# Splitting the preparation of the attention's values into prompt columns and a late sample step, in a hybrid decoder step on one Trainium2 core

## The chip, the cores and the metric

The kernel runs on one core of one Trainium2 chip. The metric is device time in microseconds (us). Engines are named as in the profile: PE is TensorE, DVE is VectorE, ACT is ScalarE, POOL is GpSimd, and SP only issues DMAs here. Each engine works through its own instructions in order, and semaphores tie the engines together. What is timed is one launch of the whole program.

## What is computed

One layer of a decoder for 1024 prompt tokens and 8 sample tokens (1032 columns in all; the samples are the last eight):

```python
hp, gate_p = _modulate(xp, c_prompt, w_cond[l], b_cond[l])
q, k, v, g_att, u, g_ssm, m_att, m_ssm = _project_in(hp, w_in[l])
o_att = _sb_prompt(q, k, v, sb_bias[l])                  # samples: _stick_breaking over a paged cache
y_ssm, sr, si = _ssm_branch(u, g_ssm, ...)               # ends in a GLU and @ w_ssm_out
# _finish:
y_att = (o_att.reshape(bsz, s, D_ATT) * jax.nn.silu(g_att)) @ w_att_out
merged = jax.nn.sigmoid(m_att) * y_att + jax.nn.sigmoid(m_ssm) * y_ssm
return _layer_norm(DEEPNORM_ALPHA * x + gate * (merged @ w_out), ln_g, ln_b)
```

The change concerns the left factor of the product with `w_att_out`: attention output times SiLU gate, which has to stand in SBUF, split in a high and a low part, before that product begins.

## The kernel before

All big products run as *jobs*: 128 output features for all 1032 columns, 8 input tiles x 3 column chunks of 344 x 3 products of high and low parts, 72 matmuls (L141, tile `pj`). A job takes the first and last two input tiles chunk by chunk, so its first 18 matmuls use tiles 0 and 1, the next 36 tiles 2 to 5, the last 18 tiles 6 and 7. The order on PE is written out by hand: `Stream.weave` spreads a list of small steps evenly over the jobs that are queued (down to a remainder `until`), and calls each step between two matmuls. The order on the other engines is left to the framework's scheduler, which goes by the order in which the code emits instructions and by its own estimate of times.

The end of the kernel has four phases of PE work: GLU (8 jobs), `ssm_out` (8 jobs), `att_out` (8 jobs) and `finish` (9 row blocks, L1397). Between them stand these pieces.

- *Late values* (`LateValues`): four of the eight cache pages of the samples' attention are weighted and summed here, in 34 steps. Step n (n < 32) loads tile `l_t` number n: DVE copies one element of the newest result into the tile (L865, so that the load does not start early), POOL issues an indirect DMA of 512 KB (L866). It then works up tile n-2: a DVE product (L884) and a DVE sum (L885). The last step adds the partial sums (L888) and ACT's queue writes the samples' attention output to `d_o` in DRAM (L889). NLATE steps are woven into the GLU, the others into `ssm_out` until LATE jobs are left of it: before 26 steps, then 8 steps over the first three jobs.
- *Gate steps* (`gate_steps`, 8 of them, over `ssm_out`): a product with a part of `w_cond` (L343, tile `gp`) whose operand is loaded into a `wc` tile (L327), split by ACT (L334, `wchi`) and by DVE (L335, `wclo`). Step n loads part n+2 and splits part n+1.
- *`open_a`* (8 steps, L1276 to L1289): for each of 8 feature tiles, load two halves of the attention output (`x` and `olo`, L1278) and the gate (`sga`, L1279), add (L1280), multiply (L1281); load the samples' rows from `d_o` (`orow`, L1283, SP's queue), transpose them on PE (`otp`, L1285), multiply (L1286); then split all 1032 columns (ACT L234, DVE L235). The gate steps and these steps are woven together over the last five jobs of `ssm_out`.
- Tiles `l_t`, `wc`, `olo`, `sga` (and `w_out` tiles later) share one ring of four SBUF buffers, tag `wc`: a tile can be loaded when the tile four allocations before it is used up. Tile `x` has a ring of two.
- Weights of the next job are loaded by SP's queue (L105), rounded by ACT (L108) and their low part made by POOL (`wlo`, L109). The results of `ssm_out` leave PSUM by DVE (L1261), those of the GLU by ACT (L1243) and DVE (L1244) and are then split (L234, L235).

Of the kernel before, what the change touches and what calls it, by code (L numbers as in the profile page):

```python
# [9 lines left out]
F32 = mybir.dt.float32  # L10
F32R = mybir.dt.float32r
I32 = mybir.dt.int32
AF = mybir.ActivationFunctionType
ALU = mybir.AluOpType
# [3 lines left out]
NP, NS, NT = 1024, 8, 1032  # L18
NC3, CW = 3, 344
KT = 8  # L20
# [8 lines left out]
MM = 146.0  # L29
# [4 lines left out]
HURRY = 400  # L34
# [3 lines left out]
QUEUES = "sasssasss"  # L38
PACE = 155
VP = 4  # L40
NLATE = 26
GS = "v"
LATE = 5.0
AHEAD = 2
DRAIN = 1.6
TWO_PI = 6.283185307179586
# [35 lines left out]
def blk(i, w=128):  # L82
    return slice(w * i, w * i + w)
# [141 lines left out]
def weaved(a, b):  # L225

    n = [((i + 0.5) / len(x), j, s) for j, x in enumerate((a, b)) for i, s in enumerate(x)]
    return [s for _, _, s in sorted(n, key=lambda e: e[:2])]


def split_act(k, pool, src):
    hi = pool.tile([128, NT], F32R, tag="hi", bufs=KT, name="ahi")
    lo = pool.tile([128, NT], F32R, tag="lo", bufs=KT, name="alo")
    k.nc.scalar.copy(hi, src)  # L234
    k.nc.vector.tensor_tensor(lo, src, hi.bitcast(F32), ALU.subtract)  # L235
    return hi, lo
# [301 lines left out]
class Attention:  # L538
# [130 lines left out]
    def turn(self, p, h, m, j):  # L669

        k, nc, pool = self.k, self.k.nc, self.pool
        PE, ACT, DVE = nc.tensor, nc.scalar, nc.vector
        w = [self.w[p, h, 2 * m + e][0] for e in range(2)]
        tp = self.ps.tile([128, 4, 128], F32, tag="wt", name="tp")
        if j < m:
            hi, lo = (pool.tile([128, 4, 128], F32R, tag=n, bufs=LAG + 1, name=n) for n in ("wthi", "wtlo"))
        else:
            hi, lo = self.diag
        order = (0, 1) if j < m else (1, 0)
        for a in order:  # L680
            for e in range(2):
                if j < m or (a, e) != (1, 0):
                    PE.transpose(tp[:, 2 * order[a] + e], w[e][:, blk(2 * j + a)], k.ident)  # L683
        with k.tc.high_priority(HURRY):
            s = slice(0 if j < m else 1, 4)
            ACT.copy(hi[:, s], tp[:, s])  # L686
            DVE.tensor_tensor(lo[:, s], tp[:, s], hi[:, s].bitcast(F32), ALU.subtract)  # L687
        return hi, lo
# [501 lines left out]
class Merge:  # L1190
# [77 lines left out]
    def open_a(self):  # L1268

        k, nc = self.k, self.k.nc  # L1270
        self.a_guard = self.pool("seta", "right")
        pa = self.a_guard.__enter__()
        self.act_a = []

        def one(f):
            t = self.load(k.d_a[f, 0], "x", NP)  # L1276
            o, s = (self.ld.tile([128, NP], F32, tag="wc", bufs=4, name=n) for n in ("olo", "sga"))
            nc.sync.dma_start(o, k.d_a[f, 1])  # L1278
            nc.sync.dma_start(s, k.d_sa[f])  # L1279
            nc.vector.tensor_tensor(t[:, 0:NP], t[:, 0:NP], o, ALU.add)  # L1280
            nc.vector.tensor_tensor(t[:, 0:NP], t[:, 0:NP], s, ALU.mult)  # L1281
            ob = self.ld.tile([NS, 128], F32, tag="orow", bufs=2, name="orow")
            nc.sync.dma_start(ob, k.d_o[:, blk(f)])  # L1283
            tp = k.psg.tile([128, 512], F32, tag="g", name="otp")
            nc.tensor.transpose(tp[:, 0:NS], ob, k.ident[0:NS, 0:NS])  # L1285
            nc.vector.tensor_tensor(t[:, NP:NT], tp[:, 0:NS], k.sgs[:, f], ALU.mult)  # L1286
            self.act_a.append(split_act(k, pa, t))

        return [(110, None, lambda f=f: one(f)) for f in range(KT)]  # L1289

    def att_out(self):
        k, nc = self.k, self.k.nc
# [160 lines left out]
def stickbreak_s5_kernel(ctx: ExitStack, tc: tile.TileContext, io, out):  # L1453
    nc = tc.nc
    k = Ctx()
# [55 lines left out]
    S = k.stream = Stream(k)  # L1511
# [108 lines left out]
    mg = Merge(k, io, out)  # L1620
# [8 lines left out]
    late = lv.steps()  # L1629
    S.weave(late[:NLATE])  # L1630
    S.drain()
    mg.g_guard.__exit__(None, None, None)
    mg.open_gate()
    mg.ssm_out()
    S.weave(late[NLATE:], LATE * KT * 9 * MM)
    S.weave(weaved(mg.gate_steps(), mg.open_a()))
    mg.s_guard.__exit__(None, None, None)
    mg.att_out()
    mg.open_out()
# [60 lines left out]
def build(nc, arrays):  # L1700
    from concourse import mybir as _mybir
    io = {n: nc.dram_tensor("in_" + n, v.shape, _mybir.dt.from_np(v.dtype), kind="ExternalInput").ap()
          for n, v in arrays.items()}
    out = {n: nc.dram_tensor("out_" + n, s, F32, kind="ExternalOutput").ap() for n, s in _OUTS}
    with tile.TileContext(nc, schedule_with_timeline_sim=True) as tc:
        stickbreak_s5_kernel(tc, io, out)
# [12 lines left out]
```

## Time and profile before

| | us |
|---|---|
| median of 3 runs (lowest to highest) | 1623.29 (1622.94 to 1626.74) |
| profiled execution, time | 1634.07 |
| profiled execution, span from first to last instruction | 1632.4 |

In the profiled execution PE is busy 92% of the span, DVE 75%, POOL 56%, ACT 45%. Times below count from the start of the span. A row of a timeline reads: start, duration, engine, line, operation, out<-in; in brackets the time in which the engine stood idle before it and what ended that. `PEclk` is the clock that PE was granted, 1.00 being 2.4 GHz and 0.50 1.2 GHz.

### The profile page before, as it was taken

Reading aid. Unit: us, or ns where it says so; the run is one execution under the profiler, and the core shown is the slowest. Engines: PE = TensorE matmul, PEld = TensorE weight load, DVE = VectorE, ACT = ScalarE, POOL = GpSimd, SP = SyncE. Lnnn points to the kernel's source line nnn. Section 1 sums busy time; section 2 is a strip of 40 time slices with the busy share of each in tenths; the row PEclk is TensorE's granted clock in tenths of the full one; section 3 lists DMA queues with packets and bytes.
Section 4 is the critical chain, followed back from the end, with each engine's and each line's share of the span. In section 5 each row is a group of like instructions: output and inputs, shape, how many; then the busy total and the mean of one; then the engine's idle time right before and its main releaser. Section 6 shows DMA issues by size and latency. Waiting matters only on the chain.

```text
span 1632.4 us, 25533 instructions
## 1 busy us (share of the span) xinstructions
PE 1496.4 (92%) x9321; PEld 1416.0 (87%) x9321; DVE 1220.2 (75%) x1717; ACT 737.4 (45%) x1360; POOL 909.0 (56%) x744
## 2 busy tenths in 40 slices
PE   8899999999999999999899898987988785999997
PEld 4689999999999999999889798987788785899885
DVE  4558888888888888734989888786489985844566
ACT  3557777777677767633333333333432212311200
POOL 1738787868787777564655555572276540132164
PEclk9999999999999999999999999998999987999999
DMA  9323433334343434347988878773556677854322
GB/s 348 108 87 86 105 102 96 100 95 113 94 113 87 119 92 106 116 142 246 289 282 258 290 231 268 264 234 80 161 169 195 211 257 256 329 190 144 116 79 91
DMA packets 176731, 275.47 MB, mean 169 GB/s; under 512 B 46395, under 2 KB 119867, under 8 KB 176477
## 3 DMA queue, kind: packets, MB, share of 16 engines
q1 hardware_dynamic: 150555, 180.40, 36.2%
q0 software_dynamic: 23456, 84.95, 16.1%
q10 hardware_dynamic: 2594, 8.49, 1.9%
q8 instruction: 73, 1.20, 0.3%
q14 instruction: 53, 0.43, 0.1%
HBM read 196.77 MB, written 66.24 MB: 161 GB/s over the span
## 4 chain that ended last, share of the span: by engine, by line
PE 48%; DVE 23%; DMA 10%; issue 6%; ACT 3%; SPq 3%; POOL 3%; DVEq 0%; POOLq 0%; ACTq 0%
PE pj L141 30%; PE f L1397 6%; PE o L700 4%; PE z L654 3%; DVE s_sc L828 3%; PE tp L683 3%; DVE ke L665 3%; DVE vs L636 2%; DVE be L666 2%; DMA tt<-gtt 1%; DVE s_t L823 1%; DMA l_t<-in_cache_v,l_idx 1%; SPq L956 1%; POOL l_t L866 1%; DMA s_t<-in_cache_k,s_idx 1%
## 5 line engine op out<-in xcount | busy, mean ns | idle before, releaser
L141 PE MATMUL pj<-ahi,whi 128*128 128x344 f32 x2112 | 698.9, 332 | 47.8 <-ACT u L970 20.3
L141 PE MATMUL pj<-alo,whi 128*128 128x344 f32 x2112 | 689.3, 328 | 7.9 <-DVE alo L1220 4.7
L141 PE MATMUL pj<-ahi,wlo 128*128 128x344 f32 x2112 | 584.2, 329 | 9.2 <-POOL wlo L109 9.2
L141 PEld LDWEIGHTS pj<-ahi,whi 128*128 128x128 f32 x2112 | 408.4, 193 | 56.8 <-ACT u L970 21.3
L141 PEld LDWEIGHTS pj<-alo,whi 128*128 128x128 f32 x2112 | 408.5, 193 | 12.2 <-DVE alo L1220 5.6
L141 PEld LDWEIGHTS pj<-ahi,wlo 128*128 128x128 f32 x2112 | 384.7, 193 | 11.4 <-POOL wlo L109 9.9
L665 DVE TENSOR_TENSOR_SCAN ke<-ke,eye 128x896 f32<-128x896 f32 (+7 forms) x128 | 219.6, 1716 | 92.9 <-ACT ke L655 92.8
L109 POOL TENSOR_TENSOR wlo<-w,whi 128x1024 fp32r<-128x1024 f32 x53 | 135.6, 2559 | 220.4 <-ACT whi L108 220.0
L108 ACT CAST whi<-w 128x1024 fp32r<-128x1024 f32 x90 | 94.9, 1054 | 130.1 <-PE pj L141 98.5
L655 ACT ACTIVATE ke<-z,nhb 128x448 f32<-128x448 f32 (+2 forms) x192 | 111.9, 583 | 81.3 <-PE z L654 79.3
L666 DVE TENSOR_TENSOR be<-be,ke 128x896 f32<-128x896 f32 (+7 forms) x128 | 120.5, 941 | 12.9 <-ACT wthi L686 0.5
L828 DVE SCALAR_TENSOR_TENSOR s_sc<-s_t,s_q,s_sc 128x512 f32<-128x512 f32 x126 | 109.8, 871 | 17.8 <-DMA s_t<-in_cache_k,s_idx 11.7
L656 ACT ACTIVATE be<-z,hb 128x448 f32<-128x448 f32 (+2 forms) x192 | 110.7, 577 | 0.0
L807 POOL DMA_INDIRECT s_t<-in_cache_k,s_idx x64 | 71.4, 1115 | 39.2 <-issue 11.4
L683 PE MATMUL tp<-ident,be 128*128 128x128 f32 x576 | 88.9, 272 | 0.0
L493 POOL TENSOR_TENSOR pt<-tab 128x256 f32<-128x256 f32 x64 | 79.1, 1236 | 3.1
L1520 ACT ACTIVATE gate<-pj 128x344 f32<-128x344 f32 x72 | 33.0, 460 | 101.2 <-PE pj L141 92.0
L492 POOL TENSOR_TENSOR pr<-tab 128x256 f32<-128x256 f32 x32 | 28.2, 880 | 90.3 <-DMA tab<-d_tab 75.7
L109 DVE TENSOR_TENSOR wlo<-w,whi 128x1024 fp32r<-128x1024 f32 x37 | 63.0, 1703 | 15.0 <-ACT whi L108 15.0
L686 ACT CAST wthi<-tp 128x512 fp32r<-128x512 f32 x96 | 56.7, 591 | 33.1 <-PE tp L683 30.8
L687 DVE TENSOR_TENSOR wtlo<-tp,wthi 128x512 fp32r<-128x512 f32 x96 | 65.4, 681 | 6.7 <-ACT wthi L686 6.5
L654 PE MATMUL z<-kl,qs 128*128 128x448 f32 (+2 forms) x192 | 66.2, 345 | 4.0 <-DMA kl<-kl 4.0
(314 smaller groups left out, 2764.8 us busy)
## 6 DMA issues: line engine op xcount, KB each, us to landing
w<-in_w_in SPq DMA_DIRECT2D x38, 512.0 KB
w<-in_w_in POOLq DMA_DIRECT2D x26, 512.0 KB, 6.2
wc<-in_w_cond SPq DMA_DIRECT2D x24, 512.0 KB
d_a<-ox SPq DMA_DIRECT2D x128, 64.0 KB
gst<-d_gg SPq DMA_DIRECT2D x8, 576.0 KB
x<-in_xr SPq DMA_DIRECT2D x9, 512.0 KB
xt<-in_xt SPq DMA_DIRECT2D x8, 516.0 KB
d_ma<-gate SPq DMA_DIRECT2D x8, 516.0 KB
```

Of the source, the lines that this page charges most:

```text
L108: nc.scalar.copy(whi, w32)
L109: self.eng.tensor_tensor(wlo, w32, whi.bitcast(F32), ALU.subtract)
L141: PE.matmul(ps[c], w[:, blk(t)], x[:, cs(c)], start=(t == 0 and i == 0), stop=(t == KT - 1 and i == 2))
L493: POOL.tensor_tensor(t1, c, d, ALU.mult)
L654: nc.tensor.matmul(z[:, 0:wide], st["q", h][:, blk(i)], x[:, s:s + wide], start=j == 0, stop=j == 1)
L655: nc.scalar.activation(ke[:, s:s + cw], z[:, 0:cw], AF.Sigmoid, bias=k.nhb[:, hd:hd + 1], scale=-0.125)
L656: nc.scalar.activation(be[:, s:s + cw], z[:, 0:cw], AF.Sigmoid, bias=k.hb[:, hd:hd + 1], scale=0.125)
L665: nc.vector.tensor_tensor_scan(rev, rev, self.eye[:, NP - n:][:, ::-1], 0.0, ALU.mult, ALU.add)
L666: nc.vector.tensor_tensor(be, be, ke[:, 1:n + 1], ALU.mult)
L683: PE.transpose(tp[:, 2 * order[a] + e], w[e][:, blk(2 * j + a)], k.ident)
L828: DVE.scalar_tensor_tensor(sc, t, q[:, d - d0:d - d0 + 1], sc, op0=ALU.mult, op1=ALU.add)
L1397: PE.matmul(pp[c], a[:, token(i)], w[:, blk(c, 512)], start=(t == 0 and a is ah and w is wh), stop=(t == KT - 1 and a is al))
```

## The change

`open_a` makes only the 1024 prompt columns. A new function `samples_a` makes the eight sample columns of all eight tiles: one load of `d_o` into a tile of the `wc` ring, eight transposes into one PSUM tile, one product, and sixteen small splits. Its load is emitted when 1.6 jobs of `ssm_out` are left, its transposes when 0.8 job is left. NLATE goes from 26 to 20, and the 14 late steps that remain are woven together with the gate steps and the prompt steps over the first 6.4 jobs of `ssm_out` (LATE from 5.0 to 1.6).

```diff
-NLATE = 26
+NLATE = 20
-LATE = 5.0
+LATE = 1.6
@@
-        def one(f):
-            t = self.load(k.d_a[f, 0], "x", NP)
+        def prompt(f):
+            t = self.load(k.d_a[f, 0], "x", NP)[:, 0:NP]
             o, s = (self.ld.tile([128, NP], F32, tag="wc", bufs=4, name=n) for n in ("olo", "sga"))
             nc.sync.dma_start(o, k.d_a[f, 1])
             nc.sync.dma_start(s, k.d_sa[f])
-            nc.vector.tensor_tensor(t[:, 0:NP], t[:, 0:NP], o, ALU.add)
-            nc.vector.tensor_tensor(t[:, 0:NP], t[:, 0:NP], s, ALU.mult)
-            ob = self.ld.tile([NS, 128], F32, tag="orow", bufs=2, name="orow")
-            nc.sync.dma_start(ob, k.d_o[:, blk(f)])
-            tp = k.psg.tile([128, 512], F32, tag="g", name="otp")
-            nc.tensor.transpose(tp[:, 0:NS], ob, k.ident[0:NS, 0:NS])
-            nc.vector.tensor_tensor(t[:, NP:NT], tp[:, 0:NS], k.sgs[:, f], ALU.mult)
-            self.act_a.append(split_act(k, pa, t))
-
-        return [(110, None, lambda f=f: one(f)) for f in range(KT)]
+            nc.vector.tensor_tensor(t, t, o, ALU.add)
+            nc.vector.tensor_tensor(t, t, s, ALU.mult)
+            hi = pa.tile([128, NT], F32R, tag="hi", bufs=KT, name="ahi")
+            lo = pa.tile([128, NT], F32R, tag="lo", bufs=KT, name="alo")
+            nc.scalar.copy(hi[:, 0:NP], t)
+            nc.vector.tensor_tensor(lo[:, 0:NP], t, hi[:, 0:NP].bitcast(F32), ALU.subtract)
+            self.act_a.append((hi, lo))
+
+        return [(0, None, lambda f=f: prompt(f)) for f in range(KT)]
+
+    def samples_a(self):
+
+        k, nc = self.k, self.k.nc
+        ob = self.ld.tile([NS, NP], F32, tag="wc", bufs=4, name="orow")
+        nc.sync.dma_start(ob, k.d_o)
+        tp = k.psg.tile([128, 512], F32, tag="g", name="otp")[:, 0:64].rearrange("p (f s) -> p f s", f=KT)
+        t = self.ld.tile([128, KT, NS], F32, tag="orow", bufs=1, name="os")
+
+        def turn():
+            for f in range(KT):
+                nc.tensor.transpose(tp[:, f], ob[:, blk(f)], k.ident[0:NS, 0:NS])
+            with k.tc.high_priority(HURRY):
+                nc.vector.tensor_tensor(t, tp, k.sgs, ALU.mult)
+                for f in range(KT):
+                    hi, lo = (x[:, NP:NT] for x in self.act_a[f])
+                    nc.scalar.copy(hi, t[:, f])
+                    nc.vector.tensor_tensor(lo, t[:, f], hi.bitcast(F32), ALU.subtract)
+
+        return [(900, None, turn)]
@@
-    S.weave(late[NLATE:], LATE * KT * 9 * MM)
-    S.weave(weaved(mg.gate_steps(), mg.open_a()))
+    S.weave(weaved(late[NLATE:], weaved(mg.gate_steps(), mg.open_a())), LATE * KT * 9 * MM)
+    S.weave(mg.samples_a())
```

Worked out from `weave`, in jobs of `ssm_out` from its start: before, the last late step comes at 2.67, the gate steps at 3.29, 3.88 and so on to 7.41, the first `open_a` step (and with it the first transpose) at 3.59. After, the gate steps come at 0.21, 1.03, 1.86 and so on to 5.78, the prompt steps at 0.62, 1.45 and so on to 6.19, the late steps at 0.41, 0.83 and so on to 5.99, and the transposes of the samples at 7.2.

## Rows read from the trace of the kernel before

**Rows 1.** Who waited for whom, PE alone, 1190 to 1540: total, times, longest

```profile
PE otp L1285 <- DMA orow<-d_o: 17.7, 1, 17.7
PE pj L141 <- POOL wlo L109: 9.2, 2, 4.9
PE pj L141 <- ACT ahi L234: 6.7, 1, 6.7
PE gp L343 <- DVE x L1286: 3.2, 1, 3.2
PE gp L343 <- DVE wclo L335: 1.7, 2, 1.1
```

**Rows 2.** Busy time by stretch: stretch, length, busy (instructions) per engine, PEclk, DMA share, GB/s

```profile
1196.00:1292.60 96.60, 87.40 (x514) 86.83 (x513) 92.73 (x96) 23.14 (x33) 61.81 (x35) 0.91 0.56 178
1292.60:1352.70 60.10, 45.32 (x266) 44.04 (x264) 50.80 (x64) 9.83 (x11) 23.62 (x17) 0.89 0.80 260
1352.70:1430.20 77.50, 62.32 (x351) 58.45 (x352) 51.53 (x62) 21.75 (x22) 10.31 (x4) 0.89 0.83 298
1430.20:1520.60 90.40, 90.40 (x577) 90.40 (x577) 38.39 (x41) 15.82 (x15) 24.36 (x8) 1.00 0.50 164
1520.60:1632.40 111.80, 101.17 (x436) 81.38 (x434) 71.87 (x147) 8.90 (x16) 46.40 (x33) 0.97 0.26 88
```

**Rows 3.** Timeline of PE where `ssm_out` meets the GLU's last split

```profile
1301.66 0.32 PE L141 MATMUL pj<-ahi,wlo 128*128 128x344 f32 x1
1308.72 0.66 PE L141 MATMUL pj<-ahi,whi 128*128 128x344 f32 x1 [6.75 <-ACT ahi L234]
```

**Rows 4.** Timeline of PE around its longest wait

```profile
1344.65 0.32 PE L141 MATMUL pj<-alo,whi 128*128 128x344 f32 x1
1344.80 0.48 PE L141 MATMUL pj<-ahi,wlo 128*128 128x344 f32 x2
1362.98 0.27 PE L1285 MATMUL otp<-ident,orow 8*128 8x8 f32 x1 [17.71 <-DMA orow<-d_o]
...
1363.64 0.49 PE L141 MATMUL pj<-ahi,whi 128*128 128x344 f32 x1
1363.92 0.49 PE L141 MATMUL pj<-alo,whi 128*128 128x344 f32 x1
...
1366.58 0.32 PE L141 MATMUL pj<-ahi,wlo 128*128 128x344 f32 x1
1366.73 0.32 PE L141 MATMUL pj<-ahi,whi 128*128 128x344 f32 x1
```

**Rows 5.** Timelines of POOL, DVE, ACT and SP: the last late load to the samples' rows

```profile
1340.95 0.94 POOL L866 DMA_INDIRECT l_t<-in_cache_v,l_idx  x1 [0.74 <-DVE l_t L865]
...
1352.50 0.22 DVE L888 TENSOR_TENSOR l_acc<-l_acc 128x64 f32<-128x64 f32 x1
...
1352.75 0.33 ACTq L889 DMA_DIRECT2D d_o<-l_acc  x1
...
1358.80 0.63 SPq L1283 DMA_DIRECT2D orow<-d_o  x2
```

**Rows 6.** By line, all or most of the trace: count, duration min/median/max ns, first to last start

```profile
L884 DVE TENSOR_TENSOR l_t<-l_t,l_sc x32: 1207/1214/8223, 1204.1 to 1349.0; 128x1024 f32<-128x1024 f32 x32
L1280 DVE TENSOR_TENSOR x<-x,olo x8: 1212/1224/3417, 1355.4 to 1422.2; 128x1024 f32<-128x1024 f32 x8
L1261 DVE TENSOR_TENSOR m<-pj,m x24: 498/508/517, 1311.1 to 1431.0; 128x344 f32<-128x344 f32 x24
L1285 PE MATMUL otp<-ident,orow x8: 223/223/271, 1363.0 to 1426.5; 8*128 8x8 f32 x8
L1219 ACT CAST ahi<-ygs x8: 197/235/347, 1157.1 to 1187.9; 128x8 fp32r<-128x8 f32 x8
L1220 DVE TENSOR_TENSOR alo<-ygs,ahi x8: 104/156/2405, 1158.1 to 1192.0; 128x8 fp32r<-128x8 f32 x8
```

**Rows 7.** Late products (L884) by stretch, columns as in group 2, DVE alone

```profile
1196.00:1292.60 96.60, 31.73 (x18) 0.91 0.56 178
1292.60:1352.70 60.10, 22.28 (x14) 0.89 0.80 260
```

**Rows 8.** Timelines of DVE, SP, PE: the gate's first operand, and loads through the ring

```profile
1289.68 1.20 DVE L885 TENSOR_REDUCE l_acc<-l_t 128x8 f32<-128x1024 f32 x1
...
1313.85 0.38 SPq L327 DMA_DIRECT2D wc<-in_w_cond  x1
...
1322.63 1.21 DVE L335 TENSOR_TENSOR wclo<-wc,wchi 128x1024 fp32r<-128x1024 f32 x1
...
1340.73 0.40 PE L343 MATMUL gp<-wchi,csplit 128*128 128x512 f32 x1
...
1349.58 0.37 SPq L1278 DMA_DIRECT2D olo<-d_a  x1
...
1391.07 0.38 SPq L327 DMA_DIRECT2D wc<-in_w_cond  x1
...
1414.63 0.32 SPq L1279 DMA_DIRECT2D sga<-d_sa  x1
```

**Rows 9.** Timeline of POOL ahead of the first wait of PE for `wlo`

```profile
1232.42 0.97 POOL L866 DMA_INDIRECT l_t<-in_cache_v,l_idx  x1 [4.05 <-DVE l_t L865]
1233.70 1.31 POOL L866 DMA_INDIRECT l_t<-in_cache_v,l_idx  x1 [0.31 <-issue]
1235.03 2.35 POOL L109 TENSOR_TENSOR wlo<-w,whi 128x1024 fp32r<-128x1024 f32 x1
```

## The prediction

> **What bounds the kernel now.** I read the waits of PE first, then the busy time by stretch, then the timelines around the longest wait. In the last 440 us PE hardly stands still except in five places, and one is far the longest: 17.7 us before the first transpose of the samples' rows [rows 1]. The stretches say what that is worth. From 1430.2 on (`att_out`, eight jobs in 90.4 us, so 11.3 us each) PE is busy without a gap, and in `finish` it is busy for 101 of 112 us [rows 2]: whatever brings the start of `att_out` forward brings the end forward by as much. Before it, in 1196 to 1292.6 (the GLU), PE is busy for 87.4 of 96.6 us and DVE for 92.7, so there DVE has hardly any slack; in 1292.6 to 1430.2 (`ssm_out`) PE has 107.6 of 137.6 us and DVE 102.3 [rows 2]. I place the start of `ssm_out` at 1292.6 because 57 matmuls of its first job, 0.157 us apart (90.4 us for the 576 of eight jobs), fit in before the wait that ends at 1308.72 for the GLU's last split [rows 3]; 57 is where tile 7 is first used.
>
> The timeline shows how the long wait comes about. PE's order reaches the first transpose at 1345.3, but DVE adds the last late partial sums only at 1352.5, ACT's queue writes `d_o` at 1352.75, SP's queue issues the load of the rows at 1358.80, and PE goes on at 1362.98 [rows 4, 5]. The order by hand assumed the late values done at 2.67 jobs; on the chip DVE was some 20 us late. Behind the transpose everything on PE is queued, though `ssm_out` does not need the samples.
>
> **The change part by part.**
>
> *The wait goes from its place.* Gone are 17.7 us, the 3.2 us in which a gate product waits for a PSUM bank held by a transpose's product (L1286), and the two short waits for `wclo` (1.7 us) that follow from the same crowding [rows 1]: 22.6 us. After the long wait nine matmuls run 0.29 us apart, at the lower level of the clock (1.2 GHz), not 0.157 us as before it and from 1366.6 on [rows 4], which is another 1.2 us; with a little of the same behind the 3.2 us wait it makes 24.5 us. If nothing took its place, `att_out` would start at 1430.2 - 24.5 = 1405.7.
>
> *The samples' step.* Eight transposes at 0.22 us (as before, so no difference), one DVE product, sixteen small splits. The nearest rows are the GLU's sample columns of the same size: 0.235 us on ACT and 0.156 us on DVE [rows 6], so 8 x 0.235 = 1.9 us of ACT with DVE following. They run beside 0.8 job (9.0 us) of `ssm_out` matmuls and are needed 12 matmuls into `att_out`; hidden, and about 4 us if that cover went. DVE loses eight products of 0.155 us and gains about as much: nothing.
>
> *What the transposes wait for now.* PE meets them at 7.2 jobs. Let T be the end of the last late sum. From T to the first transpose took 1362.98 - 1352.7 = 10.3 us [rows 5]; then come 1.8 us of transposes and 9.0 us of matmuls, so `att_out` starts at T + 21.1 or at 1405.7, whichever is later. Everything hangs on T, which the change puts behind more work: the last late step moves from 2.67 to 5.99 jobs, with seven of the eight prompt steps and all gate steps emitted ahead of it.
>
> *T by DVE's work.* DVE was busy for 92.73 + 50.80 = 143.5 us from 1196 to T [rows 2]. Of the 51.5 us after it, nearly all now stands ahead of T, but for one prompt step (3 x 1.22), the PSUM exits of the last two jobs (6 x 0.51), two `w_out` splits of the same shape as the prompt's (2 x 1.2) and the transposes' products (1.2), 10.4 us together [rows 2, 6]: 41.1 us. The sum is 184.6 us. The late steps cost DVE the same wherever they are emitted; of the 32 products 14 already ran after 1292.6 [rows 7], which is what 20 steps in the GLU leave. So NLATE takes no work from the GLU that was done there; it takes away the backlog. At the share that DVE kept in the GLU, 0.96, T = 1196 + 192 = 1388; at its share over 1196 to 1352.7, 0.916, T = 1397.5; never idle, 1380.6. I take 0.94, since in the later stretch DVE fed on one stream and stood waiting for its loads, and now has three: T = 1392.
>
> *T by the ring of four buffers.* The first gate operand (w0) needs the slot of late tile 16, whose sum is the 17th and ended near 1290 [rows 8]. From w0 on, the last late tile is the 32nd allocation (8 `wc`, 12 `l_t`, 12 `olo` and `sga`), 31 turns later, and from its issue to T took 1352.5 - 1340.95 = 11.6 us [rows 5]. The ring's pace was 20 turns from the first `olo` (1349.58) to the last `sga` (1414.63), 3.25 us each, and in its best part nine turns from 1391.07 to 1414.63, 2.6 us each [rows 8]: T = 1290 + 31 x 3.25 + 11.6 = 1402 or, at 2.6, 1382. The middle agrees with 1392.
>
> *The gate's first step* moves from 3.29 to 0.21 jobs. Before, its operand was loaded at 1313.85, when the ring let it, and `wclo` was ready at 1323.8, 10 us later [rows 8], long before PE came at 1340.73. Now PE comes at about 1295, and the load can go at 1290: ready at 1300 or later. So PE will wait here, 5 to 15 us, with `ssm_out` behind it; but in that time the GLU's last split ends, and the wait of 6.75 us for it at 1308.72 [rows 3] is swallowed. I count the two as equal; the ends are a gain of 7 (operand in time, GLU caught up) and a loss of 21 (operand as late as before: 28 us, less the 7.4 us at the split). This is the new wait that I expect first. It costs the end little as long as T decides.
>
> *The GLU.* Two waits of 4.3 and 4.9 us for `wlo` come from POOL standing at late loads whose copy DVE has not made [rows 1, 9]. With 2.5 instead of 3.25 loads a job both may go; none to 9 us plus some 5 at the lower clock. For T this counts only as DVE's work does, so I enter nothing and keep it for the range.
>
> *A rule weighed.* Late products take 1.21 us at the median, but 31.73 / 18 = 1.76 us on average in the GLU, where POOL is busy 64% of the time, and 22.28 / 14 = 1.59 in the next stretch, at 39% [rows 2, 6, 7]. The Trainium skill (SBUF — State Buffer, "SBUF: two separate sides") says that DVE and GpSimd share a port pair under an exclusive lock, so that a DVE instruction with two SBUF inputs waits out a GpSimd instruction that reads SBUF. By that, late products spread over all of `ssm_out`, where POOL is less busy, would cost some 0.2 us less each, 14 x 0.2 = 3 us off T. The rows agree in direction; I leave these 3 us out of the sum.
>
> *SP's queue.* The one load of `d_o` waits on SP until the write has landed. Behind it stand weights and operands of `att_out`. The load is issued at T + 6 [rows 5]; a weight behind it, if its way to the low part is as long as that of the gate's operand, 10 us [rows 8], is ready at T + 16, and `att_out` starts at T + 21: covered, with 5 us to spare.
>
> **Sum.** T = 1392 by DVE and by the ring; 1392 + 21.1 = 1413, against 1405.7 from PE's own work. `att_out` starts 17 us earlier. The profiled execution (1634.07, of which 1632.4 span) would come to 1617; it lies 10.8 us above the median of the runs, so I take the difference off the median: 1623.3 - 17 = 1606.
>
> **The rivals.**
>
> 1. *PE alone decides.* DVE hardly idles (T = 1381 to 1384), and the GLU's waits go: `att_out` at 1395 to 1405, a gain of 24 to 35, 1588 to 1599. For: the GLU's DVE share of 0.96. Against: in 1352.7 to 1430.2 DVE kept only 0.66, waiting for operands, with DMA already at a share of 0.83 [rows 2].
> 2. *The wait comes back nearly whole* at 7.2 jobs: the late chain runs at the share of 1292.6 to 1352.7, 0.845. T = 1414, `att_out` 1435; with a part of the mix, from 1420 on. 1613 to 1628, within 0.3% for most of it. This is also the case that the change only moves the wait.
> 3. *Slower: the ring.* Five allocations a turn of 0.82 job, interleaved, so that a `wc` tile waits for a late tile that waits for DVE. If a tile's turn goes over (1409 - 11.6 - 1290) / 31 = 3.5 us, `att_out` starts later than before; at 3.8 us, T = 1419, `att_out` 1440, a loss of 10: 1633. Gate steps that wait for `wclo` one after another would show it.
>
> **How the numbers follow.** The forecast (1599 to 1614) 0.5, rival 1 0.18, rival 2 0.22, rival 3 0.1. A measurement of this kernel can tell about 0.3% (4.9 us) from no change. Faster by more: 0.5 + 0.18 and a quarter of rival 2, 0.74. Within: 0.16. Slower: rival 3, 0.1. The range 1592 to 1625 leaves out the far part of rival 1 and rival 3.
>
> **What would show it.** Right: no wait at 3.6 jobs; one wait of PE at its first gate product near 1295 to 1305 in place of the wait at the split; one wait of some 8 us at the transposes, followed by `att_out` near 1413; DVE above 0.9 busy from 1196 until the last late sum near 1392. Wrong, if the last late sum lies near its transposes' place without a wait (rival 1), or if the gate's products wait at several steps by more than 3 us each (rival 3), or if prompt splits hold up the first job of `att_out`, which I took as done by then.

## The result

The changed kernel takes 1632.94 us (median), the kernel before 1623.91 us on the same chip: a ratio of 1.0059 with a 95% interval of 1.0042 to 1.0077. It is slower by about 9 us, where 1606 was forecast. The profiled execution of the changed kernel took 1634.53 us, 1632.8 of it span.

The waits of PE in the changed kernel, 1190 to 1540 (total, times, longest), answer to [rows 1]:

```profile
PE gp L343 <- ACT wchi L334: 14.7, 4, 9.3
PE otp L1300 <- DMA orow<-d_o: 10.8, 1, 10.8
PE pj L141 <- POOL wlo L109: 9.4, 5, 2.6
PE gp L343 <- DVE wclo L335: 6.2, 5, 2.3
```

Gone are the wait of 17.7 us in the middle of `ssm_out` and the 6.7 us for the GLU's last split. In their place stand a wait for the samples' rows at the new transposes (10.8) and waits of the gate products (14.7 and 6.2). The waits for `wlo` are as long as before, in more and shorter pieces.

Busy time by stretch, columns as in [rows 2]; the GLU, `ssm_out` to the last late sum, from there to `att_out`, `att_out`; then 1196 to the last late sum in one piece:

```profile
1194.00:1290.80 96.80, 87.50 (x516) 86.09 (x515) 86.06 (x92) 23.27 (x33) 63.45 (x34) 0.94 0.53 173
1290.80:1407.50 116.70, 94.67 (x534) 89.53 (x534) 99.24 (x113) 26.75 (x29) 37.23 (x21) 0.91 0.82 297
1407.50:1430.70 23.20, 13.50 (x79) 13.51 (x80) 12.16 (x21) 5.26 (x13) 3.83 (x1) 0.78 0.75 276
1430.70:1521.10 90.40, 90.40 (x577) 90.40 (x577) 36.52 (x39) 15.83 (x15) 23.55 (x8) 1.00 0.45 144
...
1196.00:1407.50 211.50, 180.18 (x1043) 173.63 (x1042) 183.99 (x204) 49.47 (x61) 98.68 (x53) 0.93 0.70 242
```

From `att_out` on nothing has changed. DVE is the column to look at: busy for 86.06 of the GLU's 96.8 us, where it had 92.73 of 96.6 before [rows 2], and for 99.24 of the 116.7 us after it.

Timelines of PE, DVE, ACT's queue and SP's queue of the changed kernel, in order of time; they answer to [rows 3 to 5]:

```profile
1292.90 0.32 PE L141 MATMUL pj<-ahi,wlo 128*128 128x344 f32 x1
1302.57 0.80 PE L343 MATMUL gp<-wchi,csplit 128*128 128x512 f32 x1 [9.35 <-ACT wchi L334]
...
1407.26 0.21 DVE L888 TENSOR_TENSOR l_acc<-l_acc 128x64 f32<-128x64 f32 x1
1407.50 0.33 ACTq L889 DMA_DIRECT2D d_o<-l_acc  x1
1413.30 0.29 SPq L1294 DMA_DIRECT2D orow<-d_o  x1
1417.20 0.99 PE L1300 MATMUL otp<-ident,orow 8*128 8x8 f32 x8 [10.77 <-DMA orow<-d_o]
...
1418.57 0.49 PE L141 MATMUL pj<-alo,whi 128*128 128x344 f32 x1
1418.86 0.49 PE L141 MATMUL pj<-ahi,wlo 128*128 128x344 f32 x1
```

The last late sum ends at 1407.5, not at 1392, and `att_out` starts at 1430.7, practically where it did before (1430.2). By these two executions the change does nothing; by the medians it loses 9 us. Both have to be explained.

### The profile page after: what moved, and what is told of

It reads as the page before. It is cut to its first block, busy times and chain, and to the rows that moved or that the text cites. A ratio compares the mean times of both kernels' runs of the same rounds, so it can differ in the third digit from the quotient of the medians.

```text
span 1632.8 us, 25533 instructions
## 1 busy us (share of the span) xinstructions
PE 1495.9 (92%) x9321; PEld 1415.4 (87%) x9321; DVE 1217.1 (75%) x1718; ACT 736.8 (45%) x1368; POOL 915.3 (56%) x744
## 4 chain that ended last, share of the span: by engine, by line
PE 50%; DVE 22%; DMA 12%; issue 6%; ACT 3%; POOL 2%; SPq 1%; DVEq 0%; ACTq 0%; POOLq 0%
PE pj L141 32%; PE f L1416 6%; PE o L700 4%; PE z L654 3%; DVE ke L665 3%; PE tp L683 3%; DVE s_sc L828 3%; DVE vs L636 2%; DMA l_t<-in_cache_v,l_idx 2%; DMA s_t<-in_cache_v,s_idx 2%; DMA s_t<-in_cache_k,s_idx 2%; DVE be L666 1%; DVE l_t L884 1%; DVE m L1244 1%; DVE s_t L823 1%
## 5 line engine op out<-in xcount | busy, mean ns | idle before, releaser
L141 PEld LDWEIGHTS pj<-ahi,wlo 128*128 128x128 f32 x2112 | 384.5, 193 | 12.2 <-POOL wlo L109 10.8
L665 DVE TENSOR_TENSOR_SCAN ke<-ke,eye 128x896 f32<-128x896 f32 (+7 forms) x128 | 223.1, 1743 | 92.4 <-ACT ke L655 92.1
L866 POOL DMA_INDIRECT l_t<-in_cache_v,l_idx x32 | 48.0, 1500 | 78.6 <-DVE l_t L865 62.3
L492 POOL TENSOR_TENSOR pr<-tab 128x256 f32<-128x256 f32 x32 | 24.4, 762 | 89.3 <-DMA tab<-d_tab 79.3
```

The costliest lines, as they stand in the source:

```text
L141: PE.matmul(ps[c], w[:, blk(t)], x[:, cs(c)], start=(t == 0 and i == 0), stop=(t == KT - 1 and i == 2))
L665: nc.vector.tensor_tensor_scan(rev, rev, self.eye[:, NP - n:][:, ::-1], 0.0, ALU.mult, ALU.add)
```

## The experiments

Executions differ by some us from their first stage on, so I count from the GLU's start: S is the end of PE's last short wait there (1194.2 in the profile of before, 1192.5 after). T is the write of `d_o`, A the start of `att_out` (10.0 us before its first result leaves PSUM). "Woven" means that the late steps are mixed with gate and prompt steps, "first" that they come ahead of them, as in the kernel before. All times in us; the time is the median of the run's executions, the ratio is to the kernel before on the same chip, where it was measured. T-S and A-S come from one profiled execution each; in e3_no_d_o, e9_seq20 and e10_split_wide that one lay 7 to 8 us under the median of its run. e0_before, e12_after and e6_ring3 are one execution each.

| run | NLATE, order | T-S | A-S | time | ratio, 95% interval |
|---|---|---|---|---|---|
| before | 26, first | 158.5 | 235.9 | 1623.91 | 1 |
| e0_before | 26, first | 155.5 | 229.2 | 1621.33 | |
| after | 20, woven | 215.0 | 238.1 | 1632.94 | 1.0042 to 1.0077 |
| e12_after | 20, woven | 212.3 | 235.7 | 1630.40 | |
| e1_split | 26, first | 156.4 | 225.1 | 1618.44 | 0.9920 to 0.9981 |
| e5_nlate26 | 26, woven | 202.6 | 227.6 | 1621.93 | 0.9961 to 1.0010 |
| e9_seq20 | 20, first | 174.5 | 232.9 | 1631.11 | 1.0014 to 1.0058 |
| e3_no_d_o | 20, woven | 210.4 | 227.9 | 1625.06 | 0.9972 to 1.0014 |
| e4_late_idle | 20, woven | 194.6 | 219.8 | 1611.10 | 0.9891 to 0.9959 |
| e6_ring3 | 20, woven | 233.4 | 256.2 | 1650.41 | |
| e7_staged | 20, woven | 212.8 | 232.3 | 1623.14 | 0.9967 to 1.0015 |
| e11_thin_olo | 20, woven | 220.4 | 240.7 | 1635.50 | 1.0042 to 1.0095 |
| e8_split_staged | 26, first | 185.2 | 237.5 | 1633.29 | 1.0025 to 1.0061 |
| e13_ahead3 | 20, first | 173.8 | 232.0 | 1626.84 | 0.9986 to 1.0030 |
| e14_nlate23 | 23, first | 175.3 | 233.0 | 1623.01 | 0.9975 to 1.0013 |
| e16_nopace | 20, first | 176.2 | 234.3 | 1629.41 | 1.0000 to 1.0041 |
| e17_after_nopace | 20, woven | 221.4 | 243.9 | 1635.91 | 1.0043 to 1.0082 |
| e10_split_wide | 26, first | 158.5 | 222.3 | 1616.60 | 0.9917 to 0.9960 |
| e15_nlate30 | 30, first | 157.6 | 219.3 | 1610.88 | 0.9895 to 0.9942 |
| e18_nlate34 | 34, first | 153.4 | 217.1 | 1611.61 | 0.9911 to 0.9950 |

From A to the end of the span every one of these profiles takes 202.2 us (202.19 to 202.25). So an execution's time is S, plus A-S, plus a constant, and S lies ahead of the first late product.

**How typical was the profile?** e0_before and e12_after are the two kernels once more, with a profile each.

> The kernel before once more, unchanged, for a second profile: its first one (1634.1) lay 10 us above the median of its runs (1623.9), and the changed kernel's (1634.5) 2 us above its own (1632.9). Theory (the 9 us between the medians come from the stretch that the change touches): the second profile lies near 1624, the GLU starts within 2 us of 1194 and ssm_out to the start of att_out is 8 to 10 us shorter than the 137.6 us of the first. Rival (they come from elsewhere): ssm_out lasts 136 to 139 us again and the difference lies before 1194 or in the GLU.

> The changed kernel once more, for a second profile. Theory (its stretch from the last wait at the GLU's start to the start of att_out is steady): 236 to 240 us, as in the first (238.1), against 229.2 in the second profile of the kernel before; the last late sum 213 to 217 us after the GLU's start. Rival (it scatters as that of the kernel before did, 229 and 236): outside of that.

Waits of PE in e0_before, same view as [rows 1]:

```profile
PE otp L1285 <- DMA orow<-d_o: 13.1, 1, 13.1
PE pj L141 <- POOL wlo L109: 9.3, 2, 4.7
PE pj L141 <- ACT ahi L234: 5.9, 1, 5.9
```

The long wait is 13.1 us here, not 17.7, and `att_out` starts 229.2 us after S, not 235.9. The GLU starts 6.0 us earlier too (S at 1188.2, not 1194.2), where the theory allowed 2. So of the 12.7 us between the two executions about half lies ahead of the GLU. The changed kernel shows 238.1 and 235.7, the second a little under what was expected, as its T-S of 212.3 is. Against 229.2 the change is 6.5 to 9 us later, about the 9 us of the medians; against 235.9 it is level to 2 us later. The first profile lies 10 us above the median of its kernel's runs and the second 4.7 us below (1625.99 on its chip), so the truth is probably in between; two profiles can't place all of the 9 us.

**The parts apart.** The change has three: the split with its late sample step, NLATE 20 for 26, and the weaving. e1_split keeps the split alone; e5_nlate26 and e9_seq20 put one of the other two back each.

```diff
 e1_split (against the changed kernel)
-NLATE = 20
+NLATE = 26
-    S.weave(weaved(late[NLATE:], weaved(mg.gate_steps(), mg.open_a())), LATE * KT * 9 * MM)
+    S.weave(late[NLATE:], 5.0 * KT * 9 * MM)
+    S.weave(weaved(mg.gate_steps(), mg.open_a()), LATE * KT * 9 * MM)
 e5_nlate26: the first pair of lines alone; e9_seq20: the second edit alone
```

> The sample step apart, as in the change, but late values placed as before: 26 steps in the GLU, 8 over the first three jobs of ssm_out, then gate and prompt steps alone over the next 3.4 jobs, samples in the last 1.6. Theory (what eats the gain is that late values, prompt and gate steps now share one ring of buffers and one DVE up to the last late step): the last late sum comes at 1352 as before, no wait at the samples' transposes, att_out starts 15 to 20 us earlier than before, 1604 to 1609. Rival (prompt and gate steps alone need their time: ring turns of 3.25 us from 1350 on, 21 of them): gate products wait, att_out starts at 1411 to 1425, 1605 to 1619. Rival 2 (the samples' step itself costs what it saves): no gain, 1620 to 1626.

> The changed kernel with NLATE back at 26: the GLU as before, 8 late steps woven with gate and prompt steps instead of 14. Theory (six late tiles fewer in the shared ring, at 3.1 us a turn, and 14 us less of DVE there): the last late sum 12 to 18 us earlier than in the changed kernel, the wait at the transposes gone, 1618 to 1622. Rival (the GLU's backlog comes back and delays the first gate operand and the split at the border by as much): 1628 to 1634.

> The split alone (late steps first, over three jobs, then gate and prompt steps), but with NLATE 20, so that 14 late steps stand in the three jobs instead of 8. With the runs at NLATE 26 it parts the two edits. Theory (NLATE 20 leaves DVE without work in the GLU, busy 0.89 there against 0.95 at 26, some 6 us of late work that then follow behind): DVE busy 0.87 to 0.90 in the GLU, the last late sum 6 to 14 us later than in the split alone, 1624 to 1630. Rival (weaving the late steps with the others is what costs, NLATE by itself nothing): within 3 us of the split alone, 1616 to 1621.

The four corners: 26 first 0.9951, 26 woven 0.9985, 20 first 1.0036, 20 woven 1.0059. The split gains 8 us. Going from 26 to 20 loses 12 to 14 us in either order, well outside the intervals. Weaving loses 4 to 6 us with either number; there the intervals overlap, so this part is weaker. e1_split came out in its first rival's range: no wait at the transposes, but 13.7 us at the gate products. e5_nlate26 came close to its theory, 10 to 12 us off T and the wait at the transposes down to 2.8, but the first gate product, now woven in early, waits longer than anything in the kernel before:

```profile
PE gp L343 <- ACT wchi L334: 23.1, 1, 23.1
```

Busy time of e1_split, GLU and GLU's end to T:

```profile
1190.60:1287.60 97.00, 87.93 (x509) 87.37 (x510) 91.93 (x100) 23.70 (x34) 62.25 (x35) 0.90 0.56 180
1287.60:1347.00 59.40, 47.84 (x281) 46.26 (x280) 51.78 (x64) 9.93 (x12) 25.07 (x17) 0.90 0.82 268
```

and of e9_seq20:

```profile
1186.00:1283.00 97.00, 88.39 (x526) 86.98 (x527) 87.08 (x96) 23.80 (x34) 65.03 (x34) 0.95 0.56 181
1283.00:1360.50 77.50, 58.21 (x324) 55.53 (x322) 59.40 (x76) 11.86 (x14) 27.55 (x18) 0.87 0.74 247
```

To T, DVE's work is nearly the same, 143.7 and 146.5 us; its idle time is 12.7 and 28.0. Of the 18 us by which T is later with 20 steps, 15 are DVE standing still. What it stood for (waits of DVE, S to T; first e1_split, then e9_seq20):

```profile
DVE l_t L884 <- DMA l_t<-in_cache_v,l_idx: 10.2, 6, 3.8
```

```profile
DVE l_t L884 <- DMA l_t<-in_cache_v,l_idx: 20.2, 9, 4.8
```

But with the late steps first T is not what PE waits for: A comes 69 and 58 us after it. Of the 7.8 us by which A-S is longer in e9_seq20, 5.6 are the wait for the GLU's last split (waits of PE; first e1_split, then e9_seq20):

```profile
PE pj L141 <- ACT ahi L234: 5.2, 1, 5.2
```

```profile
PE pj L141 <- ACT ahi L234: 10.8, 1, 10.8
```

Timeline of DVE in e9_seq20:

```profile
1293.62 1.23 DVE L335 TENSOR_TENSOR wclo<-wc,wchi 128x1024 fp32r<-128x1024 f32 x1 [2.12 <-ACT wchi L334]
...
1300.09 0.50 DVE L1244 TENSOR_TENSOR m<-m,sig 128x344 f32<-128x344 f32 x1
```

The split of the gate's first operand, waiting for ACT, stands ahead of the GLU's last result in DVE's order; in e1_split it comes at 1317.25, 15 us behind it (1301.94). Some 6 of the 14 us between these two runs the profiles don't show; e9_seq20's is the fastest of its ten executions.

**What sets T in the changed kernel?** Candidates were the load of `d_o`, DVE's work, the ring of four buffers, and DMA.

```diff
 e3_no_d_o (the samples' rows come from other data, ready long before)
-        nc.sync.dma_start(ob, k.d_o)
+        nc.sync.dma_start(ob, k.d_q)
 e4_late_idle (tiles of steps after the GLU are neither weighted nor summed)
+        if n < NLATE - AHEAD:
             nc.vector.tensor_tensor(t, t, self.sc..., ALU.mult)
             nc.vector.tensor_reduce(self.acc[:, j, 8 * c:8 * c + 8], t, ..., ALU.add)
+        else:
+            nc.vector.tensor_copy(self.acc[:, j, 8 * c:8 * c + 8], t[:, :, 0])
 e6_ring3: bufs=4 becomes bufs=3 wherever the tag is "wc"
 e7_staged (olo and sga are loaded into the tiles that later hold ahi and alo)
-            o, s = (self.ld.tile([128, NP], F32, tag="wc", bufs=4, name=n) for n in ("olo", "sga"))
+            o, s = (x[:, 0:NP].bitcast(F32) for x in (hi, lo))
 e11_thin_olo (one half of the attention output: 16 of 1024 columns loaded, the first one added)
-            nc.sync.dma_start(o, k.d_a[f, 1])
+            nc.sync.dma_start(o[:, 0:16], k.d_a[f, 1, :, 0:16])
 e8_split_staged: e1_split with the edit of e7_staged
```

> The changed kernel, with the samples' rows loaded from the queries' buffer, which is full long before, in place of the attention output: the transposes no longer wait for the late values (the samples' result is left wrong, all work is the same). Theory (the last late sum sets the start of att_out through that wait, 10.8 us and 10 matmuls at the lower clock): no wait there, att_out 12 us earlier, the time 10 to 12 us under the changed kernel's. Rival (the last prompt parts, split at 1416, would hold att_out anyway): 0 to 5 us.

Without the chain through `d_o` the time falls by 8 us (11 by the ratios), at or a little under the theory's 10 to 12. PE still waits 5.5 us at the transposes, since the load, whose tile comes from the ring, is issued only at 1394.92 and the transposes start at 1400.29. The wait at the transposes is real, and not the whole story.

> The changed kernel with the products and sums of late values left out in the steps woven into ssm_out (a copy of 64 numbers stands for each pair); loads, buffers and order stay. DVE loses about 14 x 2.3 = 32 us. Theory (the ring of four buffers sets the pace: turns of 3.1 us, of which a late tile's time on DVE is a small part): the last late step ends 5 to 12 us earlier, the time falls by 5 to 12 us, gate products still wait. Rival (DVE's work sets the pace): the last late step ends some 25 us earlier, att_out is held by PE alone (near 1406 in the profile), the time falls by 20 to 25 us.

T comes 18 to 20 us earlier and the time drops to 1611, the 22 us of the rival. Busy time of e4_late_idle from 1283.1 to T:

```profile
1283.10:1380.70 97.60, 87.63 (x526) 84.69 (x525) 63.55 (x96) 25.82 (x28) 35.09 (x20) 0.95 0.92 328
```

DVE's work in this stretch is 36 us less than the 99.24 of the changed kernel, T only 20 us earlier: DVE's work counts for most, but something else holds T too.

> The changed kernel with the shared ring at three buffers instead of four (late values, gate parts, prompt parts, the samples' rows, and w_out parts later). Theory (the ring sets the pace after the GLU): a turn goes from 3.1 towards 4.1 us, the last late sum comes 15 to 32 us later, the time rises by as much. Rival (DVE's work or the DMA engines set the pace): it moves by under 4 us.

> The changed kernel, but the second half of the attention output and the gate are loaded into the two tiles that the split writes afterwards, so that 16 of the 37 tiles leave the ring; DVE's work and the bytes moved stay the same. Theory (the ring sets the pace): the last late sum 10 to 16 us earlier, gate products hardly wait, 1617 to 1623. Rival (DVE's work sets the pace): the last late sum moves by under 4 us, 1629 to 1634. In neither can ssm_out fall under some 118 us, since its transfers take 113 us of all DMA engines (139.9 us at a share of 0.81).

With a buffer less T is 18 us later, as the ring theory has it (one execution). With 16 of the 37 tiles out of the ring, T moves by nothing (212.8 against 215.0 and 212.3), and the time still falls by 10 us: what goes are waits of PE. Waits of PE in e7_staged:

```profile
PE pj L141 <- POOL wlo L109: 10.8, 7, 3.4
PE gp L343 <- ACT wchi L334: 9.3, 1, 9.3
...
PE gp L343 <- DVE wclo L335: 2.5, 3, 1.7
PE otp L1300 <- DMA orow<-d_o: 2.3, 1, 2.3
```

The first gate product waits as long as before, but the later ones no longer (14.7 to 9.3, 6.2 to 2.5). So the four buffers tie the gate's operands to the late tiles. That they don't hold T this run can't show, since the edit does a second thing: 20 of 24 prompt loads are now issued by S + 135, against 5 in the changed kernel, and what early prompt loads cost the last run of this group shows.

> The changed kernel with the second half of the attention output loaded for 16 columns only and its first column added in place of the whole (that part of the result is left out; buffers, their order and DVE's instructions stay). 4 MB, some 12 us of all DMA engines, leave ssm_out. Theory (transfers at a share of 0.82 to 0.92 make every turn of the ring longer): the last late sum 8 to 14 us earlier, the time 8 to 14 us under the changed kernel's. Rival (DVE's work and order set it): under 4 us.

4 MB less to load, the DMA share down from 0.82 to 0.74 (S + 97 to T), and T is later, if anything: it isn't the amount of bytes. Nor does relief of the ring carry over to the better order:

> The run with late values placed as before and the sample step apart, with the same staging as in the run above: only late tiles and gate parts use the ring. Theory (the ring holds the gate products, 13.7 us of waits): the waits at the gate go, 1606 to 1612. Rival (the DMA engines, busy 0.94 of the time from the last late sum to the start of att_out, are the bound by then): within 3 us of that run, 1615 to 1621.

Both expectations were wrong. There the prompt loads, no longer held by the ring, go out from S + 105 instead of S + 153 (all but two); DMA is busy at a share of 0.92 from the GLU's end to T, T is 29 us later than in e1_split, and the gain is gone. Of the 29 us, 24 are work that DVE now does ahead of T (168.1 against 143.7 us), most of it the prompt parts. The ring was also a brake that kept the prompt loads behind the late tiles.

So of these edits only less work on DVE brought T forward by much (e4_late_idle), and a smaller ring put it back by as much (e6_ring3); how the two share it with four buffers is open.

**Why do 20 steps cost so much?** Before, 18 products were done when the GLU ended [rows 7]; with 20 steps it is 17. The issue of the late loads differs more. POOL's timelines around the GLU's end, e9_seq20 (20 steps):

```profile
1283.40 1.70 POOL L866 DMA_INDIRECT l_t<-in_cache_v,l_idx  x1 [1.43 <-DVE l_t L865]
...
1300.92 0.95 POOL L866 DMA_INDIRECT l_t<-in_cache_v,l_idx  x1 [2.75 <-DVE l_t L865]
1302.17 1.58 POOL L866 DMA_INDIRECT l_t<-in_cache_v,l_idx  x1 [0.30 <-issue]
1304.06 0.94 POOL L866 DMA_INDIRECT l_t<-in_cache_v,l_idx  x1 [0.30 <-issue]
```

and e10_split_wide (26 steps, S 2.8 us earlier):

```profile
1285.32 1.67 POOL L866 DMA_INDIRECT l_t<-in_cache_v,l_idx  x1 [1.13 <-DVE l_t L865]
...
1292.57 0.98 POOL L866 DMA_INDIRECT l_t<-in_cache_v,l_idx  x1 [1.85 <-DVE l_t L865]
1295.17 0.94 POOL L866 DMA_INDIRECT l_t<-in_cache_v,l_idx  x1 [1.62 <-DVE l_t L865]
1297.97 1.70 POOL L866 DMA_INDIRECT l_t<-in_cache_v,l_idx  x1 [1.86 <-DVE l_t L865]
1299.97 0.94 POOL L866 DMA_INDIRECT l_t<-in_cache_v,l_idx  x1 [0.30 <-PE pj L141]
...
1314.23 0.95 POOL L866 DMA_INDIRECT l_t<-in_cache_v,l_idx  x1 [7.63 <-DVE l_t L865]
```

With 20 steps the last load that belongs to the GLU goes at S + 97, and none for 17.5 us; with 26 six more follow the 20th, up to S + 117 (the last five are shown), and the hole (14 us) comes behind them. Three ways to close the hole were tried: one load further ahead, three more steps, and no hold by the results of `ssm_out`.

```diff
 e13_ahead3 (against e9_seq20)
-AHEAD = 2
+AHEAD = 3
 e14_nlate23 (against e10_split_wide): NLATE = 23
 e16_nopace (against e9_seq20), e17_after_nopace (against the changed kernel): in evac of ssm_out
-            k.late.pace(m)
```

> The late steps first and NLATE 20, as in e9_seq20, but each late load is emitted three steps ahead of its product instead of two (so one product fewer is emitted in the GLU). Theory A, DVE starves because 20 paced loads are all that is there: in e9_seq20 DVE waited 20.2 us for late tiles, against 10.2 with NLATE 26, so a load that is further ahead gives about 10 us back: T 160 to 166 us after the GLU's start (174.5 in e9_seq20), 1621 to 1626. Theory B, it is only how many products are emitted before the GLU's end: T 174 to 178, 1630 to 1634.

> The split with the late steps first and room to 0.6 job, as e10_split_wide, but NLATE 23 instead of 26. Both theories: in between; the loss from 26 to 20 was 12 to 14 us, so some 6 us: T about 166, 1621 to 1625. If the loss comes only when the backlog of DVE is gone (it had 18 products done of 24 emitted with NLATE 26, and 17 of 18 with 20), 23 still leaves a backlog of three or four tiles, as many as the ring holds, and loses next to nothing: T 157 to 161, 1616 to 1619.

> As e9_seq20 (late steps first, NLATE 20), but the results of ssm_out no longer hold the late loads back: the element that DVE copies into a tile ahead of its load stays one of the GLU's last result. Pace theory: in e9_seq20 the first 20 loads were issued by 97 us after the GLU's start and the 21st only at 115, with the first exit of ssm_out, then three with each further job; without the copy of that exit the loads go on from about 100 us at the ring's pace, DVE's waits for late tiles fall from 20 us to about 10, T goes from 174.5 to about 160 after the GLU's start and the time to 1617 to 1624. Rival, the order in which the steps are emitted sets it whatever releases the loads: T 172 to 177, 1628 to 1634.

> The changed kernel with the same edit. The pace theory gives the hole after load 20 back (it was issued at 100, the 21st at 117): T 203 to 209 after the GLU's start in place of 215 and 212, 1623 to 1629. What is left would be the weaving. Rival: T 211 to 216, 1630 to 1636.

My theory fell three times, as far as T goes. Loads further ahead leave T where it was (173.8), 23 steps are as late as 20 (175.3), and without the hold T is 176.2 and 221.4. The times are less clear: 1626.84 with loads further ahead lies between the two theories, and 1623.01 with 23 steps is what was expected, half-way between 20 and 26, although T is not; that run has the wider room of e10_split_wide, which e9_seq20 has not. Timeline of DVE in e16_nopace around the hole:

```profile
1311.02 1.20 DVE L885 TENSOR_REDUCE l_acc<-l_t 128x8 f32<-128x1024 f32 x1
1312.15 0.14 DVE L860 COPY l_p<-m 128x1 f32<-128x1 f32 x1
1312.21 0.50 DVE L1244 TENSOR_TENSOR m<-m,sig 128x344 f32<-128x344 f32 x1
1312.63 0.26 DVE L865 COPY l_t<-l_p 128x1 f32<-128x1 f32 x3
1313.83 1.24 DVE L235 TENSOR_TENSOR alo<-m,ahi 128x1032 fp32r<-128x1032 f32 x1 [0.93 <-ACT ahi L234]
```

and in e10_split_wide:

```profile
1292.15 0.14 DVE L865 COPY l_t<-l_p 128x1 f32<-128x1 f32 x1
...
1294.75 0.15 DVE L865 COPY l_t<-l_p 128x1 f32<-128x1 f32 x1
...
1296.00 0.51 DVE L1244 TENSOR_TENSOR m<-m,sig 128x344 f32<-128x344 f32 x1
...
1297.55 0.14 DVE L865 COPY l_t<-l_p 128x1 f32<-128x1 f32 x1
```

The copies that let the next loads go stand in DVE's own order behind the GLU's last results (L1244), three together, with or without the hold; with 26 steps they stand one by one among them. A step emitted after the GLU has its instructions there, and DVE works in order. That is one reading. The ring is another: right behind step NLATE the code allocates the gate's first two tiles (`open_gate`), so the second load behind it takes the slot of tile NLATE. In e16_nopace the sum of that tile ends at 1312.22 (1311.02 + 1.20), 0.4 us before the three copies, so the ring alone would hold the second load as long. The first load's slot was free at 1303.75, when the two sums before that one ended; there the order must have held it. With 20, 23, 26 and 30 steps the hole follows load 20, 23, 26 and 30, which both readings give (with 23 it starts at S + 109 and is 18 us long), and no run parts them. Why T jumps between 23 and 26 isn't shown either.

**The other way.** If the place of the steps decides, more of them belong in the GLU, not fewer. The runs that follow also give the gate and prompt steps room down to 0.6 job.

```diff
 e10_split_wide (against e1_split)
-LATE = 1.6
+LATE = 0.6
 e15_nlate30, e18_nlate34 (against e10_split_wide): NLATE = 30, NLATE = 34
```

> The split alone, with gate and prompt steps over 4.4 jobs of ssm_out instead of 3.4 (until 0.6 job is left, the samples' transposes at 0.3). Theory (PE meets the gate steps faster than their operands pass the ring): the 13.7 us of waits at the gate fall to 6 or less, 1608 to 1614. Rival (the DMA engines are the bound from the last late sum on, at a share of 0.94): the wait moves to the first products of att_out or the transposes, 1616 to 1621.

> As e10_split_wide with NLATE 30 instead of 26. DVE is busy for 91.3 of the GLU's 97 us with 26 already, so there is hardly more to be had: T 154 to 159 after the GLU's start. What POOL's queue of loads does to the low parts of the weights in the GLU decides the rest: 1613 to 1622.

> As e15_nlate30 with all 34 late steps in the GLU. By the pace theory no load waits for an exit of ssm_out any more, and the late sums run at the pace of DVE and of the ring: T 145 to 155 after the GLU's start (157.6 with 30), and the gate steps find the ring free earlier: 1606 to 1613. If the GLU's own splits are held up by late products emitted ahead of them, its last wait grows (5.9 with 30) and the time is 1613 to 1622.

With 23, 26 and 30 steps the ratios are 0.9994, 0.9939 and 0.9918; with 34 it is 0.9931, not to be told from 30; the intervals of 26 and 30 overlap as well, and T is the same with both (158.5 and 157.6), so that more than 26 steps help is not shown. The wider room took the waits at the gate from 13.7 us to 5.2, as its theory said, but not the time: 1616.60 is in the rival's range and not to be told from e1_split. The kernels with 30 and 34 steps beat both others, by 11 to 13 us the one before and by 21 to 22 the changed one. Waits of PE in e15_nlate30:

```profile
PE pj L141 <- POOL wlo L109: 9.2, 2, 4.9
PE pj L141 <- ACT ahi L234: 5.9, 1, 5.9
PE gp L343 <- DVE wclo L335: 3.6, 2, 2.1
PE otp L1300 <- DMA orow<-d_o: 2.5, 1, 2.5
```

The gate products wait 3.6 us instead of the changed kernel's 20.9, the transposes 2.5 instead of 10.8 (with 26 steps 5.2 and 4.2). The border wait stays (5.9), as does `wlo`.

## Why the prediction was wrong

*DVE's work to T:* 184.6 us forecast, 183.99 measured. Right. *The share at which DVE would do it:* 0.94 forecast, 183.99 / 211.5 = 0.87 measured. This is the step that failed, and it makes T 15.5 us later (14.5 and 17.2 us counted from S, in the two profiles). It had two grounds. The first was the sentence that NLATE "takes no work from the GLU that was done there; it takes away the backlog". The count of products was nearly right (17, one of them under way at the GLU's end, against 18), but DVE was busy for 6.7 us less there, at 0.89 and not 0.96. e1_split and e9_seq20 show the same: 0.95 and 0.90 in the GLU, and 15 us more idle time to T for nearly the same work. So a backlog was worth something. The second was that behind the GLU DVE "fed on one stream and stood waiting for its loads, and now has three". With three streams it stood at 0.85 there, and in e5_nlate26, with the backlog given back, at 0.82 (86.22 of 105.6 us), no better than the 0.845 of the kernel before. Putting 26 steps back returns 10 to 12 us of T; the share over the whole way stays at 0.88.

*The ring* gave 1402 or 1382 for T. It turned in 3.12 us (31 turns from 1294.74 to 1391.50), within my two ends. But its other terms were short: the first gate operand was loaded at 1294.74, not 1290, and from the last late load to T it took 16.0 us, not 11.6. The agreement of the middle with 1392 was no second proof; it was luck.

*From T to `att_out`:* 21.1 forecast, 23.2 measured. T to the first transpose 9.7 (10.3 forecast), the transposes 0.9 (1.8), the matmuls behind them 12.6 (9.0). Of these 3.6 us, 1.3 come from ten matmuls that run 0.29 us apart after the wait, at a granted clock of 0.50 (1418.2 to 1421.0), which is 1.2 GHz; I had counted this cost in the wait that goes, and not in the one that I forecast. The other 2.3 are a slip in the place: the transposes do not stand at 7.2 jobs. `Stream.run` returns when a job is finished, so the step that was to come 0.8 job before the end comes at 7.0, with a whole job of 72 matmuls behind it; the trace has 70 records there, where 0.8 job has 58.

So 1413 + 15.5 + 2.1 = 1430.6 for the start of `att_out`; 1430.7 was measured.

*Off the median.* I took the gain off the median although the profiled execution lay 10.8 us above it. That presumes the changed kernel's profile as far above its own; it was 1.6 above (1634.53 and 1632.94). e0_before, 12.7 us shorter, shows what can be in the 10.8: an S that is 6.0 earlier, and 6.7 in A-S, 4.6 of them in the long wait. Of the 22.6 us that I counted as waits gone, 5.6 were not there in that second execution. 1606 + 17.6 + 9.2 = 1632.8.

*The rivals.* The mechanism that came true is rival 2's, the wait that comes back because DVE keeps a share near 0.85; I gave it 0.22, and 1613 to 1628, and `att_out` at 1430.7 is within its 1420 to 1435. Its price was off by the same 9 us. The time is rival 3's, but not its mechanism: the ring stayed under 3.5 us a turn, and behind the first gate product only one more waited for over 3 us (3.71 at 1385.13). The range left out the case of rival 2 and an untypical profile together.

*What held:* no wait at 3.6 jobs; the first gate product waits 9.35 us near 1302 and swallows the border wait; a wait at the transposes (8 forecast, 10.8 measured); SP's load 5.8 us after T; no wait for the sample step's splits (PE is busy for all of the 90.4 us of `att_out`). The waits for `wlo` that "both may go" stayed at 9.4 us in total. The late products, which the Trainium skill (SBUF — State Buffer, "SBUF: two separate sides") would have made shorter where POOL works less, took 1.52 us each on average behind the GLU (the 15 that start there, with POOL busy 32% of the time), against 1.59 before [rows 7]: a third of the 0.2 us, in the direction of the rule, and nothing that T shows.

## What to carry to other kernels

A backlog in front of an engine that is nearly full is no slack. Here six fewer steps emitted in the GLU left the count of finished pieces almost the same, yet at the border no load went for 17.5 us, DVE idled, and 12 to 14 us were lost in either order. Nor did several streams fill the engine: with three, DVE's share behind the GLU was about what it was with one. Before work is spread over a later stage, try the opposite too; here the split was good for 8 us, and with more late work in the early stage and wider room behind it for 11 to 13. Read the loop that places the steps before you trust a place worked out from it. Take a second profile of the kernel before where the first lies far from the median, and count only the waits that both show.

## What was unexpected

Two executions of one kernel differ in a single wait by 4.6 us (17.7 and 13.1) and in the stretch from S to `att_out` by 6.7 us (235.9 and 229.2), while from there to the end all 20 profiles agree within 0.06 us. And 4 MB less of DMA traffic in a stretch with a DMA share of 0.82 bought nothing (e11_thin_olo), while loads let out early cost 15 us (e8_split_staged against e1_split: 1633.29 and 1618.44).
